# Low parts of the first block's attention and retention weights: every other one subtracted on GpSimd

## Chip, cores and metric

One core of a Trainium2 chip runs the kernel. The metric is the device time of one execution in microseconds, as the median of several runs. TensorE (PE; its weight loads are PEld), VectorE (DVE), ScalarE (ACT), GpSimd (POOL) and SyncE (SP, which starts the DMAs) each work through an instruction list of their own and wait for each other through semaphores.

## What is computed

Two transformer blocks in fp32 on x of 256 rows by 1024. The first block has two layers: an attention layer (layer 0) and a retention layer (layer 1), each followed by a gated feed-forward layer. A vector c gives each layer six modulation vectors ("ada"). The second block is two further hybrid layers, which the change doesn't touch.

```python
def first_block(x, c, ada_w, ada_b, norm_gains, ...):
    for layer in range(2):
        shift_m, scale_m, gate_m, shift_f, scale_f, gate_f = split(silu(c) @ ada_w[layer] + ada_b[layer], 6)
        h = rms_norm(x, norm_gains[layer, 0]) * (1 + scale_m) + shift_m
        y = attn_hybrid_mixer(h, ...) if layer == 0 else retention_mixer(h, ...)
        x = x + gate_m * y
        h = rms_norm(x, norm_gains[layer, 1]) * (1 + scale_f) + shift_f
        x = x + gate_f * swiglu(h, ...)
    return rms_norm(x, final_norm)

def attn_hybrid_mixer(h, w_qkv, w_o, pos):       # 16 heads of 64
    q, k, v = heads(h @ w_qkv)
    sb = stick_breaking_attention(q[:8], k[:8], v[:8])
    mb = moba_attention(rotary(q[8:]), rotary(k[8:]), v[8:])   # one block here: causal softmax
    return concat(sb, mb) @ w_o

def retention_mixer(h, w_in, gn_gain, w_o, pos): # 4 heads
    q, k, v, g = split(h @ w_in)
    o = group_norm(retention_chunkwise(rotary(q), rotary(k) * dk ** -0.5, v)) * gn_gain
    return (silu(g) * o) @ w_o
```

## The kernel before

Every matrix product is made of three products in the reduced type fp32r, from a high and a low part of each operand: high times high, low times high, high times low. The weights arrive in fp32 in raw tiles of 128 by 2048, which SyncE loads (`raw`, L320). Two raw buffers lie in the pool `wp`, and every third raw tile goes to a buffer in `lp`. `pump` (L334) cuts each raw tile, a "chunk", into two pieces of 128 by 1024. Of each piece ScalarE makes the high part, tile `whi`, by a cast (L350), and VectorE the low part, tile `wlo`, as raw minus high part (L351). There is a ring of WB = 8 pieces. `pump` is called as TensorE's products use pieces up, so it runs ahead of them by at most eight.

The order of TensorE's instructions is written by hand: the program keeps a clock of its own (`now`) and due times of jobs (`push`, `tick`), and under `manual_schedule` TensorE's instructions stand in the order in which this recording makes them. The other engines' orders are made by a scheduler of the language. A job such as `rotary` or `causal_job` is a generator: what stands behind a `yield D_...` is recorded that many microseconds of the recorder's clock later.

Beside the gemms run background steps: the modulation vectors. `ada_steps` (L564) clears a 128 by 1024 accumulator on GpSimd (L566), loads the bias row into it (L567), and adds eight products of a 128 by 1024 weight slab with a per-partition scalar, each one a VectorE instruction (L575, "acc step"). There is one accumulator buffer, so a vector's memset waits for the split of the vector before (L491, L492). `pump` feeds such steps at a rate per chunk, `R_L0` = 2.04 in layer 0 and `R_L1` = 0.59 in layer 1.

Layer 0 (`layer0`, L823): behind the startup come the stick-breaking heads (`sb_job`, L655: tiles `sbe`, `sbs` and `aT`, the second and third of which VectorE finishes at L666, L668 and L674), while the gemm of the rotated heads' q and k runs. Its results go through `rotary` on VectorE (L616 to L619: tiles `rows` and `rt`), are transposed on TensorE (L284) and copied to qT and kT on ScalarE (L865). Then come the heads with causal softmax (`causal_job`, L621: the masked maximum on VectorE at L632, tiles `sm` and `st`, the exponential and the scaling on ScalarE, L636 and L640), while the v gemm runs, and the gemm of `w_ao`. `split` at L492 makes the low part of a head's output, tile `oTk`.

Layer 1 (`layer1`, L989): the gemms of q and k with `rotary` behind each, then those of v, then those of the gate g; the heads' group norm takes a `rstd` (L484), whose power is a GpSimd instruction on 128 by 1 (L487); then the gemm of `w_ro`. GpSimd has little else to do in the kernel: these powers, those of the other norms (L519), and the memsets.

## Time and profile before

| what | value |
| --- | --- |
| runs shown | 1473.52, 1475.32, 1475.45 us; median 1475.32 |
| the profiled execution's own time | 1474.96 us |
| its span (first to last instruction) | 1473.0 us, granted TensorE clock 0.995 on average |
| TensorE busy | 98% |
| VectorE, ScalarE, GpSimd busy | 71%, 55%, 7% |
| low parts, VectorE L351 | 450 instructions, 538.2 us |
| acc steps, VectorE L575 | 80 instructions, 102.2 us |

The profile is one execution taken apart by engine. Busy time is the sum over an engine's instructions; the idle time that counts is TensorE's, and it is told stage by stage by windows and by the timeline, in which an idle stretch of an engine stands in brackets with the work that ended it. All times in the trace are counted from the start of the span. A row of the timeline that ends in x2 is two equal instructions, one behind the other.

### The profile page before, as it was taken

The page shows a single profiled execution, that of the slowest core. Times are in us where ns is not written, and L with a number is a line of the kernel's source. Part 1 is how long each engine was busy: PE and PEld are TensorE (multiplying, and loading weights), DVE is VectorE, ACT ScalarE, POOL GpSimd, SP SyncE. Part 2 cuts the span into 40 slices and gives each one's busy share as a digit, 9 for nine tenths or more (in the row PEclk, how much of TensorE's full clock was granted, in tenths as well). Part 3 has the DMA queues.
Part 4 walks back from the last instruction along what each step waited for, and adds up shares of the span by engine and source line. Part 5 has one row for each costly group of instructions (what it writes and reads, how often), then busy time and mean ns, then how long its engine had stood idle before and what let it go on. Part 6 is the DMA issues. An engine that isn't in the chain of part 4 may idle for free.

```text
span 1473.0 us, 19815 instructions
## 1 busy us (share of the span) xinstructions
PE 1448.8 (98%) x7476; PEld 1185.7 (80%) x7476; DVE 1046.3 (71%) x1675; ACT 813.6 (55%) x1365; POOL 106.4 (7%) x88
## 2 busy tenths in 40 slices
PE   8999999999999999999999999999999999999998
PEld 6776788887887888888878888888888888888887
DVE  5688898956988848966378756565666866666664
ACT  4657556643544535655356755666445675566651
POOL 0000000000001000000012012110000201221000
PEclk9999999999999999999999999999999999999999
DMA  9757587765776646755435455455535545555452
GB/s 380 280 201 271 199 315 287 286 207 184 284 272 243 235 165 233 297 185 197 165 123 194 166 184 210 162 177 172 193 143 190 188 147 206 195 188 189 158 175 82
DMA packets 53091, 306.64 MB, mean 208 GB/s; under 512 B 7674, under 2 KB 12154, under 8 KB 20100
## 3 DMA queue, kind: packets, MB, share of 16 engines
q1 hardware_dynamic: 51988, 304.87, 57.8%
q8 instruction: 59, 0.97, 0.3%
q10 hardware_dynamic: 1008, 0.50, 0.1%
q14 instruction: 36, 0.29, 0.1%
HBM read 301.16 MB, written 1.05 MB: 205 GB/s over the span
## 4 chain that ended last, share of the span: by engine, by line
PE 88%; DVE 5%; ACT 2%; DMA 2%; POOL 1%; issue 1%; ACTq 0%; DVEq 0%; POOLq 0%
PE p L280 84%; PE p L284 4%; DVE wlo L351 2%; ACT whi L350 1%; DMA raw<-in_w_in_dram 1%; POOL qss L487 1%; POOL ss L519 0%; DMA as<-in_ada_s_dram 0%; DVE junk L527 0%; DMA sq<-in_k_sq_dram 0%; DVE res L554 0%; DMA raw<-in_w_ao_dram 0%; DVE acc L575 0%; DVE x L555 0%; ACT sm L636 0%
## 5 line engine op out<-in xcount | busy, mean ns | idle before, releaser
L280 PE MATMUL p<-whi,hT 128*128 128x512 f32 (+1 forms) x2240 | 748.1, 401 | 4.9 <-DVE hT L492 2.7
L351 DVE TENSOR_TENSOR wlo<-raw,whi 128x1024 fp32r<-128x1024 f32 x450 | 538.2, 1215 | 147.9 <-ACT whi L350 143.9
L350 ACT CAST whi<-raw 128x1024 fp32r<-128x1024 f32 x450 | 461.8, 1045 | 242.7 <-PE p L280 189.4
L280 PEld LDWEIGHTS p<-whi,hT 128*128 128x128 f32 x2240 | 422.8, 189 | 99.7 <-issue 7.3
L280 PE MATMUL p<-wlo,hT 128*128 128x512 f32 (+1 forms) x1120 | 437.6, 391 | 0.0
L280 PEld LDWEIGHTS p<-wlo,hT 128*128 128x128 f32 x1120 | 212.1, 189 | 39.2 <-issue 1.7
L280 PE MATMUL p<-hT,whi 128*128 128x512 f32 x576 | 199.2, 398 | 0.0
L280 PE MATMUL p<-hT,wlo 128*128 128x256 f32 x576 | 149.9, 281 | 0.0
L280 PEld LDWEIGHTS p<-hT,whi 128*128 128x128 f32 x576 | 103.8, 188 | 19.6
L280 PEld LDWEIGHTS p<-hT,wlo 128*128 128x128 f32 x576 | 108.7, 189 | 6.6
L575 DVE SCALAR_TENSOR_TENSOR acc<-raw,csc,acc 128x1024 f32<-128x1024 f32 x80 | 102.2, 1277 | 3.5 <-DMA raw<-in_ada_w_dram 3.2
L487 POOL TENSOR_TENSOR dss<-dss,mh 128x8 f32<-128x8 f32 (+3 forms) x36 | 56.1, 1557 | 318.2 <-DVE dss L486 318.2
L280 PE MATMUL p<-whi,al 128*128 128x512 f32 x176 | 69.5, 395 | 0.0
L280 PE MATMUL p<-wlo,ah 128*128 128x512 f32 x176 | 69.5, 395 | 0.0
L280 PE MATMUL p<-whi,ah 128*128 128x512 f32 x176 | 69.5, 395 | 0.0
L1410 DVE TENSOR_TENSOR rows<-p,dss 128x512 f32<-128x512 f32 (+3 forms) x36 | 18.5, 514 | 46.2 <-POOL dss L487 46.2
L962 ACT COPY fT<-p 128x256 f32<-128x256 f32 x72 | 26.2, 370 | 45.2 <-PE p L280 45.2
L519 POOL TENSOR_TENSOR ss<-ss,mh 128x1 f32<-128x1 f32 x14 | 13.4, 960 | 471.2 <-DVE ss L518 471.2
L280 PE MATMUL p<-whi,s 128*128 128x512 f32 x128 | 41.3, 397 | 0.0
L280 PEld LDWEIGHTS p<-wlo,ah 128*128 128x128 f32 x176 | 33.0, 187 | 8.1
L280 PEld LDWEIGHTS p<-whi,al 128*128 128x128 f32 x176 | 33.0, 187 | 8.0
L280 PEld LDWEIGHTS p<-whi,ah 128*128 128x128 f32 x176 | 33.0, 187 | 8.0
(262 smaller groups left out, 1621.1 us busy)
## 6 DMA issues: line engine op xcount, KB each, us to landing
raw<-in_w_in_dram SPq DMA_DIRECT2D x84, 1024.0 KB, 4.9
raw<-in_w_gu_dram SPq DMA_DIRECT2D x44, 1024.0 KB, 5.2
raw<-in_ada_w_dram SPq DMA_DIRECT2D x40, 1024.0 KB, 5.3
raw<-in_w_ret_dram SPq DMA_DIRECT2D x24, 1024.0 KB, 4.9
raw<-in_w_dn_dram SPq DMA_DIRECT2D x22, 1024.0 KB, 4.9
raw<-in_w_qkv_dram SPq DMA_DIRECT2D x11, 1024.0 KB, 5.7
as<-in_ada_s_dram SPq DMA_DIRECT2D x16, 512.0 KB, 10.0
raw<-in_w_ro_dram SPq DMA_DIRECT2D x8, 1024.0 KB, 6.1
```

The costliest lines, as they stand in the source:

```text
L280: self.T.matmul(out, lhsT=lhsT, rhs=rhs, start=first, stop=last, skip_group_check=skip)
L284: self.T.transpose(out, in_, self.ident)
L350: for ins in (self.A.copy(hi[:, :m * n], src), self.V.tensor_tensor(lo[:, :m * n], src, hi[:, :m * n].bitcast(F32), ALU.subtract)):
L351: self.V.tensor_tensor(lo[:, :m * n], src, hi[:, :m * n].bitcast(F32), ALU.subtract)):
L487: self.G.tensor_tensor(ss, ss, self.mh[:, :n], ALU.pow)
L519: self.G.tensor_tensor(ss[:, 0:1], ss[:, 0:1], self.mh[:, 0:1], ALU.pow)
L575: self.V.scalar_tensor_tensor(acc, r[:, j * D:j * D + D], self.sc[:, k:k + 1], acc, ALU.mult, ALU.add)
L962: A.copy(f, ps[:, 256:512])
L1410: V.tensor_tensor(d3(rows[:, :nu * 128]), d3(src), ss[:, :2 * nu, None].to_broadcast([128, 2 * nu, 64]), ALU.mult)
```

## The change

A flag `share` is false at first. It is set behind layer 0's startup and cleared ahead of the gemm of `w_ao`; set again at the head of layer 1 and cleared ahead of the gemm of `w_ro`. While it is set, `pump` gives the subtraction of the second piece of each chunk (j = 1) to GpSimd; the first stays on VectorE. The cast stays on ScalarE for both.

```diff
--- before.py
+++ after.py
@@ -249,6 +249,7 @@
         self.tc, self.nc, self.a, self.ctx = tc, tc.nc, a, ctx
         nc = tc.nc
         self.T, self.V, self.A, self.G = nc.tensor, nc.vector, nc.scalar, nc.gpsimd
+        self.share = False
         self.base = ctx.enter_context(tc.tile_pool(name="base", bufs=1))
         self.wp = ctx.enter_context(tc.tile_pool(name="wp", bufs=WB))
         self.hp = ctx.enter_context(tc.tile_pool(name="hp", bufs=1))
@@ -347,8 +348,10 @@
                 hi = self.wp.tile([128, 1024], F32R, tag="whi", name=self.nm("whi"))
                 lo = self.wp.tile([128, 1024], F32R, tag="wlo", name=self.nm("wlo"))
                 src = r[:, k * n:(k + m) * n]
+
+                sub = self.G if self.share and j % 2 else self.V
                 for ins in (self.A.copy(hi[:, :m * n], src),
-                            self.V.tensor_tensor(lo[:, :m * n], src, hi[:, :m * n].bitcast(F32), ALU.subtract)):
+                            sub.tensor_tensor(lo[:, :m * n], src, hi[:, :m * n].bitcast(F32), ALU.subtract)):
                     if self.pin:
                         self.tc.keep_in_program_order(ins)
                 v = lambda w: w[:, :m * n].rearrange("p (k n) -> p k n", n=n)
@@ -826,7 +829,7 @@
             self.ph, self.smb = p, 3
             hT, ps0 = self.startup(lp)
             self.tc.keep_in_program_order(A.preload_act_table_set("natural_log_exp_and_others"))
-            self.rate = R_L0
+            self.rate, self.share = R_L0, True
             jobs = [self.ada(lp, 0, v) for v in (2, 3, 4)]
             rope = p.tile([128, 2, 3, 32], F32, name="rope64")
             nc.sync.dma_start(rope, self.a["k_rope64"].rearrange("p (t j d) -> p t j d", t=2, j=3))
@@ -902,6 +905,7 @@
                 return tuple(x[:, k % 4, t * 128:t * 128 + 128] for x in oT[k // 4])
 
             nxt = self.res_norm(gate, lambda: self.finish(jobs[1], jobs[2])[::-1])
+            self.share = False
             self.gemm_k(ho, "w_ao", 8, nxt.epi, tail=T_AO)
         return nxt
 
@@ -993,7 +997,7 @@
             nc.sync.dma_start(rope, self.a["k_rope256"].rearrange("p (t j d) -> p t j d", t=2, j=3))
             dec = p.tile([128, 4, 384], F32, tag="dg", name="decay")
             nc.sync.dma_start(dec, self.a["k_decay"].rearrange("p (h n) -> p h n", h=4))
-            self.rate = R_L1
+            self.rate, self.share = R_L1, True
             jobs = [self.ada(lp, 1, v) for v in (2, 3, 4)]
             s4 = lambda dt=F32: p.tile([128, 4, 256], dt, tag="s4", bufs=9, name=self.nm("s4"))
             as_rows = lambda x: x.rearrange("p a b -> p (a b)").rearrange("p (t n) -> p t n", t=2)
@@ -1083,6 +1087,7 @@
                 return tuple(x[:, k % 4, t * 128:t * 128 + 128] for x in oT[k // 4])
 
             nxt = self.res_norm(gate, lambda: self.finish(jobs[1], jobs[2])[::-1])
+            self.share = False
             self.gemm_k(ho, "w_ro", 16, nxt.epi)
         return nxt
```

All later lines of the changed program stand one to five lines further down: L351 becomes L354, L575 becomes L578, rotary's L616 to L619 become L619 to L622, and so on. Thirty subtractions change engine, six in layer 0 and 24 in layer 1. TensorE's order is the same in both programs. VectorE's, ScalarE's and SyncE's are made anew by the scheduler, and change beyond the thirty. Three places follow.

VectorE, late in the stick-breaking heads of layer 0, up to the rotation of the first q rows (`rows_901`), which TensorE transposes next. `acc_800` is the first modulation vector's accumulator, `raw_808`, `raw_893` and `raw_897` its weight slabs, `aT_776` a stick-breaking head's tile. First an earlier piece of it, before:

```order
L575 SCALAR_TENSOR_TENSOR acc_800<-raw_808,csc,acc_800 128x1024
L351 TENSOR_TENSOR wlo_793<-raw_790,whi_792 128x1024
L351 TENSOR_TENSOR wlo_797<-raw_790,whi_796 128x1024
L575 SCALAR_TENSOR_TENSOR acc_800<-raw_808,csc,acc_800 128x1024
L616 TENSOR_TENSOR rows_901<-p_766,rope_645 128x512
L575 SCALAR_TENSOR_TENSOR acc_800<-raw_893,csc,acc_800 128x1024
L666 SCALAR_TENSOR_TENSOR sbs_754<-p_750,sbe_753 128x384
```

and now:

```order
L578 SCALAR_TENSOR_TENSOR acc_800<-raw_808,csc,acc_800 128x1024
L354 TENSOR_TENSOR wlo_793<-raw_790,whi_792 128x1024
L578 SCALAR_TENSOR_TENSOR acc_800<-raw_808,csc,acc_800 128x1024
L578 SCALAR_TENSOR_TENSOR acc_800<-raw_893,csc,acc_800 128x1024
L619 TENSOR_TENSOR rows_901<-p_766,rope_645 128x512
L578 SCALAR_TENSOR_TENSOR acc_800<-raw_893,csc,acc_800 128x1024
L669 SCALAR_TENSOR_TENSOR sbs_754<-p_750,sbe_753 128x384
```

The low part `wlo_797` is gone, and the second of the two acc steps on `raw_893` stands here, where before it came later. The piece that ends with the rotation's last add, before:

```order
L351 TENSOR_TENSOR wlo_886<-raw_883,whi_885 128x1024
L351 TENSOR_TENSOR wlo_890<-raw_883,whi_889 128x1024
L575 SCALAR_TENSOR_TENSOR acc_800<-raw_893,csc,acc_800 128x1024
L617 TENSOR_TENSOR rt_902<-p_766,rope_645 128x8x32
L575 SCALAR_TENSOR_TENSOR acc_800<-raw_897,csc,acc_800 128x1024
L618 TENSOR_TENSOR rt_902<-p_766,rope_645 128x8x32
L575 SCALAR_TENSOR_TENSOR acc_800<-raw_897,csc,acc_800 128x1024
L619 TENSOR_TENSOR rows_901<-rows_901,rt_902 128x512
```

and now:

```order
L354 TENSOR_TENSOR wlo_886<-raw_883,whi_885 128x1024
L578 SCALAR_TENSOR_TENSOR acc_800<-raw_897,csc,acc_800 128x1024
L620 TENSOR_TENSOR rt_902<-p_766,rope_645 128x8x32
L578 SCALAR_TENSOR_TENSOR acc_800<-raw_897,csc,acc_800 128x1024
L621 TENSOR_TENSOR rt_902<-p_766,rope_645 128x8x32
L677 SCALAR_TENSOR_TENSOR aT_776<-aT_776,strict 128x2x128
L622 TENSOR_TENSOR rows_901<-rows_901,rt_902 128x512
```

The low part `wlo_890` and the acc step on `raw_893` are gone from here, and one stick-breaking product, `aT_776`, now stands ahead of the last add instead of behind it.

GpSimd, from the first memset to the sixth low part, before:

```order
L566 MEMSET acc_800 128x1024
L519 ISA
L519 TENSOR_TENSOR ss_131<-ss_131,mh 128x1
L519 TENSOR_TENSOR ss_150<-ss_150,mh 128x1
L566 MEMSET acc_991 128x1024
L566 MEMSET acc_1226 128x1024
L566 MEMSET acc_1673 128x1024
```

and now:

```order
L354 TENSOR_TENSOR wlo_797<-raw_790,whi_796 128x1024
L354 TENSOR_TENSOR wlo_890<-raw_883,whi_889 128x1024
L569 MEMSET acc_991 128x1024
L354 TENSOR_TENSOR wlo_984<-raw_977,whi_983 128x1024
L354 TENSOR_TENSOR wlo_1028<-raw_1021,whi_1027 128x1024
L354 TENSOR_TENSOR wlo_1219<-raw_1212,whi_1218 128x1024
L569 MEMSET acc_1226 128x1024
L354 TENSOR_TENSOR wlo_1306<-raw_1299,whi_1305 128x1024
L569 MEMSET acc_1673 128x1024
```

The six low parts of layer 0 stand between what was there, and the memset of the third accumulator, `acc_1226`, now stands behind `wlo_1219`.

VectorE, at the first softmax head (tiles `sm_1098`, `st_1099`; `acc_991` is the second accumulator), before:

```order
L492 TENSOR_TENSOR oTk_1050<-p_1058,oTq_1049 128x256
L351 TENSOR_TENSOR wlo_1024<-raw_1021,whi_1023 128x1024
L351 TENSOR_TENSOR wlo_1028<-raw_1021,whi_1027 128x1024
L575 SCALAR_TENSOR_TENSOR acc_991<-raw_1031,csc,acc_991 128x1024
L492 TENSOR_TENSOR oTk_1050<-p_1065,oTq_1049 128x256
L575 SCALAR_TENSOR_TENSOR acc_991<-raw_1031,csc,acc_991 128x1024
L492 TENSOR_TENSOR oTk_1050<-p_1072,oTq_1049 128x256
L575 SCALAR_TENSOR_TENSOR acc_991<-raw_1035,csc,acc_991 128x1024
L632 ISA sm_1098,st_1099<-p_1095,causal_647 128x128
L632 ISA st_1099 128x1
L575 SCALAR_TENSOR_TENSOR acc_991<-raw_1035,csc,acc_991 128x1024
L632 ISA sm_1098,st_1099<-p_1095,causal_647 128x256
```

and now:

```order
L354 TENSOR_TENSOR wlo_1024<-raw_1021,whi_1023 128x1024
L495 TENSOR_TENSOR oTk_1050<-p_1058,oTq_1049 128x256
L495 TENSOR_TENSOR oTk_1050<-p_1065,oTq_1049 128x256
L495 TENSOR_TENSOR oTk_1050<-p_1072,oTq_1049 128x256
L578 SCALAR_TENSOR_TENSOR acc_991<-raw_1031,csc,acc_991 128x1024
L635 ISA sm_1098,st_1099<-p_1095,causal_647 128x128
L635 ISA st_1099 128x1
L578 SCALAR_TENSOR_TENSOR acc_991<-raw_1031,csc,acc_991 128x1024
L635 ISA sm_1098,st_1099<-p_1095,causal_647 128x256
L635 ISA st_1099 128x1
```

The low part `wlo_1028` is gone, and of the four acc steps that stood ahead of the head's second maximum two are left.

## Rows read from the trace of the kernel before

**Rows 1.** The page's first part: busy time of each engine over the span.
```profile
PE 1448.8 (98%) x7476; PEld 1185.7 (80%) x7476; DVE 1046.3 (71%) x1675; ACT 813.6 (55%) x1365; POOL 106.4 (7%) x88
```
**Rows 2.** Windows (start:end, length, busy time of each engine, PEclk, DMA share, GB/s).
```profile
128.00:144.00 16.00, 13.96 (x67) 9.82 (x66) 15.32 (x41) 15.43 (x45) 0.00 (x0) 1.00 0.65 215
...
375.00:530.00 155.00, 155.00 (x698) 124.22 (x697) 133.09 (x163) 74.00 (x90) 8.30 (x11) 1.00 0.70 257
```
**Rows 3.** Timeline of PE, layer 0 (start, duration; in brackets idle before, releaser).
```profile
94.62 0.66 PE L284 MATMUL p<-ident,rows 128*128 128x128 f32 x2 [3.38 <-DVE rows L619]
...
112.20 0.63 PE L284 MATMUL p<-ident,rows 128*128 128x128 f32 x4 [0.33 <-DVE rows L619]
...
131.75 0.84 PE L284 MATMUL p<-ident,sm 128*128 128x128 f32 x3 [0.70 <-ACT sm L640]
```
**Rows 4.** Windows around PE's longest idle stretch in layer 0 (PEclk: granted clock).
```profile
91.24:94.60 3.36, 0.00 (x0) 0.01 (x1) 3.36 (x5) 1.19 (x2) 0.00 (x0) 0.85 0.98 378
94.60:97.00 2.40, 2.38 (x8) 2.11 (x9) 2.02 (x4) 0.94 (x2) 0.32 (x1) 0.50 1.00 355
97.00:99.50 2.50, 2.50 (x7) 1.92 (x7) 1.19 (x3) 0.00 (x0) 0.63 (x1) 0.50 0.80 329
99.50:102.00 2.50, 2.50 (x13) 2.11 (x12) 1.27 (x3) 0.85 (x2) 0.00 (x0) 0.82 0.12 49
```
**Rows 5.** Timeline of DVE up to the same stretch's end.
```profile
75.96 1.22 DVE L351 TENSOR_TENSOR wlo<-raw,whi 128x1024 fp32r<-128x1024 f32 x1
...
84.56 0.56 DVE L666 SCALAR_TENSOR_TENSOR sbs<-p,sbe 128x384 f32<-128x384 f32 x1 [0.43 <-PE p L280]
...
87.27 2.35 DVE L351 TENSOR_TENSOR wlo<-raw,whi 128x1024 fp32r<-128x1024 f32 x2
89.54 1.28 DVE L575 SCALAR_TENSOR_TENSOR acc<-raw,csc,acc 128x1024 f32<-128x1024 f32 x1
90.74 0.42 DVE L617 TENSOR_TENSOR rt<-p,rope 128x256 f32<-128x256 f32 x1
...
93.79 0.68 DVE L619 TENSOR_TENSOR rows<-rows,rt 128x512 f32<-128x512 f32 x1
94.39 0.75 DVE L674 SCALAR_TENSOR_TENSOR aT<-aT,strict 128x256 f32<-128x256 f32 x2
```
**Rows 6.** Groups of lines by form, POOL: memset of an accumulator.
```profile
L566 POOL MEMSET acc<- 128x1024 f32 x10 | 9.6, 956 | 329.0 <-DVE accl L492 218.6 <-DMA raw<-in_ada_w_dram 88.2 <-issue 21.9
```
**Rows 7.** Timeline of POOL, two powers of layer 1, and DVE beside the second.
```profile
431.65 0.55 POOL L487 TENSOR_TENSOR bn<-bn,mh 128x1 f32<-128x1 f32 x1 [19.11 <-DVE bn L486]
435.59 1.59 POOL L487 TENSOR_TENSOR bn<-bn,mh 128x1 f32<-128x1 f32 x1 [3.39 <-DVE bn L486]
...
435.54 1.23 DVE L351 TENSOR_TENSOR wlo<-raw,whi 128x1024 fp32r<-128x1024 f32 x1
```
**Rows 8.** All of L351: ns min/median/max; below it, who waited for it.
```profile
L351 DVE TENSOR_TENSOR wlo<-raw,whi x450: 957/1220/1230, 13.5 to 1450.0; 128x1024 fp32r<-128x1024 f32 x144, 128x832 fp32r<-128x832 f32 x4, 128x768 fp32r<-128x768 f32 x2
...
  ACT whi L350: 1.1, 1
```
**Rows 9.** Timelines of DVE, ACT and PE around the second rotation of layer 0.
```profile
105.06 1.22 DVE L351 TENSOR_TENSOR wlo<-raw,whi 128x1024 fp32r<-128x1024 f32 x1
...
111.26 1.05 ACT L350 CAST whi<-raw 128x1024 fp32r<-128x1024 f32 x1 [1.24 <-DMA raw<-in_w_ao_dram]
...
113.79 0.48 PE L280 MATMUL p<-kT,qT 64*128 64x256 f32 x1 [0.55 <-ACT kT L865]
```
**Rows 10.** Timelines of DVE and ACT at the first softmax head.
```profile
120.73 0.42 DVE L632 CUSTOM_DVE_ANT_0 sm<-p,causal 128x256 f32<-128x256 f32 x1
...
122.71 0.40 ACT L636 ACTIVATE sm<-sm,st 128x128 f32<-128x128 f32 x1
```
**Rows 11.** Timelines of DVE and PE, a rotation in layer 1.
```profile
389.25 0.68 DVE L619 TENSOR_TENSOR rows<-rows,rt 128x512 f32<-128x512 f32 x1
...
392.48 0.60 PE L284 MATMUL p<-ident,rows 128*128 128x128 f32 x4
```

## The prediction

> **What bounds the kernel now.** The page's busy times come first [rows 1]: TensorE is busy for 98% of the span, and VectorE, the engine that the change relieves, for 71%. So the time can only move where TensorE stands still, or comes to. Next the windows [rows 2]: in the stretch of layer 1 shown TensorE is busy for 155.00 of 155 us, in layer 0's softmax heads for 13.96 of 16, so 2.04 us are idle there. The timeline of TensorE in layer 0 [rows 3] names the idle times: 3.38 us that end at 94.62 with the rotated rows from VectorE, 0.33 at 112.20 with the second rotation's rows, and in the softmax pieces of up to 0.70, of which ScalarE's scaled `sm` ends the longest. The clock must be read with the first of these [rows 4]: it is granted at 0.85 on average in the idle stretch, then at 0.50 while TensorE is fully busy again from 94.60 to 99.50, and at 0.82 in the next window. If in that last window it rises once from 0.5 to 1, 0.36 of its 2.50 us, 0.9 us, are at 0.5: 5.8 us at half clock (1.2 instead of 2.4 GHz), so 2.9 us of work lost.
>
> Is a low part itself late for TensorE? Over all 450 subtractions only ScalarE ever waits for one, once, for 1.1 us [rows 8]. The low parts are made ahead of need. What VectorE's subtractions cost is the place they take ahead of the rotated rows and the softmax tiles.
>
> **Two unknowns.** The trace shows no GpSimd subtraction of this size. Let t be its time. The nearest row is the memset of the same 128x1024 shape, one stream (a write): 0.956 us [rows 6]. A subtraction reads two tiles and writes one. Low bound: the memset's 0.95. High bound: three streams one behind the other, 2.85. I take two, 1.9: the write runs beside the reads, the reads one behind the other, as with a single path.
>
> The second unknown is whether VectorE's instructions wait while GpSimd's runs. The only hint is a pair of powers on 128x1 [rows 7]: alone one took 0.55 us; the other began 0.05 us behind the start of a VectorE subtraction of 1.23 us, and took 1.59, that is 0.41 longer than the rest of the subtraction (1.18) and about the sum of that rest and its own work. So GpSimd stood until VectorE was done. The other direction, VectorE standing until GpSimd is done, is not shown. I take it to hold too: one path to memory that one of the two has at a time. Then a piece moved to GpSimd costs VectorE t instead of the 1.14 us from one of its subtractions to the next (88.41 being half way in the pair that begins at 87.27 and ends before 89.54 [rows 5]), so each moved piece is 0.76 us dearer.
>
> The Trainium skill ("SBUF — State Buffer", Who interferes with whom) says that a VectorE instruction with two SBUF inputs contends with a GpSimd instruction that reads SBUF, and that whoever has the shared port pair first keeps it for the whole instruction while the other stands. The 0.55 against 1.59 us agree on GpSimd's side; no row shows VectorE's.
>
> **The change part by part.** Thirty subtractions leave VectorE. ScalarE's casts and the loads stay; their order moves.
>
> *A, the idle stretch before 94.62.* The order decides how much VectorE does ahead of `rows_901`'s last add. In the earlier piece `wlo_797` (−1.14) leaves and an acc step moves in (+1.20, 89.54 to 90.74 [rows 5]): +0.06, plus t if VectorE is held, less the 0.43 us that VectorE idles at 84.56 and can absorb. In the later piece `wlo_890` (−1.13) and that acc step (−1.20) leave and one `aT` product comes in (+0.33, from 94.39: two take 0.75, less overlap): −2.00, plus t. With holding: 0.06 + t − 0.43 − 2.00 + t = 2t − 2.37. At t = 1.9 that is **+1.43**; at 0.95 −0.47; at 2.85 +3.33. The half clock behind it I leave as it is, since the idle stretch is hardly shorter at the low bound (2.91) and longer at the others.
>
> *B, the second rotation.* `wlo_984` leaves the stretch in which VectorE makes the second rows (it is the subtraction at 105.06 or its pair [rows 9]), and its raw buffer `raw_977` is read until GpSimd is done. Behind that buffer stand a load of `w_ao`, for which ScalarE idles 1.24 us at 111.26, and the copy of kT behind it, for which TensorE waits 0.55 at 113.79 [rows 9]. Either way the shift is t − 1.14 = **+0.76**. Bounds: −0.33, the idle time at 112.20 being all there is to win, and +1.71 at t = 2.85. On SyncE the load of another weight tile now goes ahead of that of `raw_977`, some pieces ahead of use: nothing.
>
> *C, the softmax heads.* Before the first head's second maximum at 120.73 [rows 10], two acc steps and `wlo_1028` less: 2 × 1.20 + 1.14 − t = 1.64 us earlier, and ScalarE's first scaling at 122.71 can come earlier with it. TensorE has 2.04 us idle there [rows 2], on ScalarE's work, which is itself busy 15.43 of 16. I take half: **−1.0**; bounds 0 and −2.04.
>
> *D, the third accumulator.* Its memset now stands behind `wlo_1219` on GpSimd; behind the memset come SyncE's bias row, the first acc step and VectorE's small instructions after it. A memset that comes t later than it would delays acc steps that no TensorE work needs for many pieces: **0**, up to +1 if a softmax reciprocal stands behind such a waiting acc step.
>
> *E, layer 1, 24 pieces.* TensorE has no idle time to win [rows 2]. VectorE has 155 − 133.09 = 21.91 us idle in the stretch; 24 × 0.76 = 18.2 us dearer would still fit, if spread evenly. The tightest consumer is the rotation: rows done at 389.25 + 0.68 = 389.93, transposed at 392.48 [rows 11], 2.55 us to spare. Three moved pieces near it would cost 3 × 0.76 = 2.3, just inside: **0**; at t = 2.85 3 × 1.71 = 5.13, less the 2.27 for two subtractions that no longer stand ahead, less 2.55, is +0.3. The group norm's powers wait behind at most one piece, and the gate gemm lies between them and their use.
>
> Sum: +1.43 + 0.76 − 1.0 + 0 + 0 = **+1.2 us** on the profiled execution's 1474.96, so 1476.2. That execution is 0.36 below the median of the runs shown; on the median, 1475.32 + 1.2 = **1476.5**.
>
> The Trainium skill ("GPSIMD Engine Reference", 3.1 Elementwise) speaks against the change: it gives 4497 ns on GpSimd and 2293 on VectorE for a fp32 tensor_tensor of 2048 elements. Halved, an estimate from that page is t = 2.25; the sum would be 3 × 2.25 − 3.51 − (2.40 + 1.14 − 2.25) / 1.64 × 1.0, about +2.5, or 1477.8. No run here shows it.
>
> This case's own range is 1473.5 (t at 0.95 with all of C) to 1479.5 (t toward 2.85, C still won in part).
>
> **Rivals.**
>
> *F, VectorE isn't held.* The two engines share memory access finely, or only GpSimd yields. For it: no VectorE subtraction in 450 took over 1.230 us [rows 8], though GpSimd was at work beside some of them; and in the pair shown it was GpSimd that stood. Against: those GpSimd instructions were tiny. Then A is −2.00, the idle stretch 1.38 us; that may leave the clock up, −2.9; B −0.33; C −1.0: together −6.2, so **1469.1**. If the clock falls all the same, −3.3, 1472.0.
>
> *S, slower: GpSimd holds VectorE, and long.* One mechanism: each low part on GpSimd stops VectorE's two-input instructions, just ahead of the rotated rows. A and B together are 3t − 3.51; without C they pass 2.95 us, about what a measurement of this kernel can tell from no change (0.2%), from t = 2.15 on. At t = 2.85: 3.33 + 1.71, C gone (0), D +1, E +0.3, so +6.3 and **1481.7**. For it: two reads and a write are three streams, and the idle stretch before 94.62 is VectorE's alone. Against: A's two pieces may begin in VectorE's idle times or beside instructions that read one tile. By the Trainium skill's rule ("SBUF — State Buffer", Who interferes with whom) this case comes about if t is that long; the trace bears it out in one direction alone.
>
> That the change does nothing can be left out: thirty subtractions stand on GpSimd in the order.
>
> **Chances.** Forecast case (about no change) 0.42, F 0.33, S 0.25. The first lies mostly within 0.2%, a little of it above; F is faster but for a small part where the clock falls and B is not won; S is slower but for its lower edge. So faster 0.32, within 0.2% 0.40, slower 0.28. The range takes F from its full price and S to its own: 1468.5 to 1482.0.
>
> **What would show it.** GpSimd's 128x1024 subtraction at 0.95, 1.9 or 2.85 us. VectorE's two-input instructions beside it stretched or late by its length (held), or still at 1.22 and 1.28 (F). The idle stretch that ended at 94.62: 4.8 us long (forecast), under 1.5 (F), over 6 (S), and the granted clock behind it. The 2.04 us between 128 and 144 halved. Layer 1 still without idle time on TensorE. I am wrong if layer 1 gains or loses over 1 us, or if a low part is itself waited for by TensorE.

## The result, and the profile after

The changed kernel takes 1493.88 us (median of 4 runs, 1492.25 to 1494.76) beside 1474.49 us for the kernel before in the same comparison: a ratio of 1.0128, interval 1.0116 to 1.0141, or 19 us slower. That is above the range (1468.5 to 1482.0). The side on which it fell is rival S's, at three times its price.

Busy times of the whole span first, as in [rows 1]. The profiled execution took 1494.76 us, its span 1493.0.

```profile
PE 1456.3 (98%) x7476; PEld 1189.1 (80%) x7476; DVE 1065.2 (71%) x1645; ACT 811.5 (54%) x1365; POOL 188.9 (13%) x118
```

VectorE has 30 instructions fewer here and is busy 18.9 us longer. Why, the changed instructions tell: the group of the 30 on GpSimd, and then, from the views of single lines, five VectorE lines (ns min/median/max).

```profile
L354 POOL TENSOR_TENSOR wlo<-raw,whi 128x1024 fp32r<-128x1024 f32 x30 | 84.5, 2829 | 172.6 <-ACT whi L353 172.6
...
L354 POOL TENSOR_TENSOR wlo<-raw,whi x30: 2361/2816/3438, 78.1 to 534.5; 128x1024 fp32r<-128x1024 f32 x30
...
L354 DVE TENSOR_TENSOR wlo<-raw,whi x420: 957/1220/3428, 13.3 to 1469.9; 128x1024 fp32r<-128x1024 f32 x134, 128x832 fp32r<-128x832 f32 x4, 128x768 fp32r<-128x768 f32 x2
L578 DVE SCALAR_TENSOR_TENSOR acc<-raw,csc,acc x80: 1264/1278/3405, 70.0 to 622.6; 128x1024 f32<-128x1024 f32 x80
L1053 DVE TENSOR_TENSOR s<-s,gn x8: 684/1366/2881, 446.6 to 497.1; 128x512 f32<-128x512 f32 x8
...
L619 DVE TENSOR_TENSOR rows<-p,rope x12: 676/682/692, 68.0 to 417.7; 128x512 f32<-128x512 f32 x12
L1052 DVE TENSOR_SCALAR s<-p,bn x8: 799/810/812, 445.7 to 494.3; 128x512 f32<-128x512 f32 x8
```

A low part on GpSimd takes 2.36 us at least, 2.83 on average and 3.44 at most. On VectorE, three of the lines shown have instructions drawn out to 2.9 to 3.4 us; before, no subtraction took over 1.230 [rows 8]. These three read two big tiles in SBUF. The two lines that take their big operand from PSUM (`p`) are never drawn out, though three instructions of each lie wholly within a low part on GpSimd in the trace. Averages by shape give the size: 408 subtractions of 128x1024 at 1.269 instead of 1.221 us are 19.6 us, 80 acc steps at 1.448 instead of 1.277 are 13.7, together 33 us, about what the 30 subtractions that left had cost (30 × 1.14 = 34). Three lines of 128x512 with two operands in SBUF (L1053, L622 and L1075: 1.68, 1.09 and 1.41 us on average instead of about 0.69) add 18.6 us. So being held cost VectorE more than it was relieved of, by about the 18.9 us.

One hold in full, from the timelines of GpSimd, VectorE and TensorE in layer 1:

```profile
515.22 3.38 POOL L354 TENSOR_TENSOR wlo<-raw,whi 128x1024 fp32r<-128x1024 f32 x1 [2.87 <-ACT whi L353]
...
515.09 1.27 DVE L578 SCALAR_TENSOR_TENSOR acc<-raw,csc,acc 128x1024 f32<-128x1024 f32 x1
516.28 3.39 DVE L354 TENSOR_TENSOR wlo<-raw,whi 128x1024 fp32r<-128x1024 f32 x1
519.60 0.68 DVE L1075 TENSOR_TENSOR gth<-gth,s 128x512 f32<-128x512 f32 x1
...
520.34 0.47 PE L285 MATMUL p<-ident,gth 128*128 128x128 f32 x1 [3.00 <-DVE gth L1075]
```

GpSimd's piece starts at 515.22 while an acc step runs to 516.36, and ends at 518.60, 2.24 us behind that step. VectorE's next subtraction starts at 516.28 and ends at 519.67, 1.07 behind GpSimd's end. Each stands until the other is done. Behind VectorE stands the product `gth`, and TensorE waits 3.00 us for it. This agrees, now in both directions, with the Trainium skill's rule ("SBUF — State Buffer", Who interferes with whom) on the shared port pair.

TensorE's idle times, from its timeline in both layers, and windows of stretches with and behind them (columns as in [rows 2, 3]):

```profile
86.31 0.92 PE L281 MATMUL p<-sbs,sq 128*128 128x256 f32 x4 [1.56 <-DVE sbs L671]
...
97.76 0.63 PE L285 MATMUL p<-ident,rows 128*128 128x128 f32 x4 [3.52 <-DVE rows L622]
...
113.64 0.63 PE L285 MATMUL p<-ident,rows 128*128 128x128 f32 x4 [1.32 <-DVE rows L622]
115.67 0.70 PE L281 MATMUL p<-kT,qT 64*128 64x256 f32 x2 [0.99 <-ACT kT L868]
...
463.34 1.22 PE L281 MATMUL p<-s,raT 128*128 128x512 f32 x1 [4.08 <-ACT s L1059]
```
```profile
94.20:97.80 3.60, 0.08 (x2) 0.07 (x2) 3.60 (x7) 1.53 (x2) 0.00 (x0) 1.00 0.82 264
97.80:100.40 2.60, 2.60 (x14) 2.20 (x15) 2.20 (x4) 0.59 (x1) 0.92 (x1) 1.00 1.00 413
...
118.50:122.80 4.30, 4.30 (x11) 2.75 (x10) 4.30 (x11) 0.00 (x0) 0.00 (x0) 0.50 0.89 332
463.00:468.00 5.00, 4.66 (x9) 3.04 (x10) 5.00 (x4) 4.56 (x6) 4.07 (x3) 0.50 0.49 194
520.00:527.00 7.00, 6.66 (x19) 5.44 (x20) 7.00 (x7) 5.44 (x7) 5.10 (x3) 0.55 0.68 269
...
375.00:530.00 155.00, 147.92 (x640) 116.93 (x639) 138.00 (x134) 64.96 (x82) 68.98 (x33) 0.96 0.64 236
```

Layer 1, gapless before [rows 2], now has two idle stretches, 4.08 and 3.00 us, each with a stretch at half clock behind it, and TensorE is busy for 147.92 of the 155 us instead of all of them. TensorE's own instructions, one by one, tell where the 20 us came: the first transpose of layer 0's norm began at 163.18 before and at 169.41 now (+6.2, of which 1.4 stood there before the first moved piece); the one at 507 before, some way into layer 1's gate gemm, comes 19.4 later, and from there on that moves by no more than about 1.5 us. So layer 1 lost 13 us in this execution. The two idle stretches are 7.1 of them (155 less 147.92); the half clock behind them is the rest.

The first idle stretch of layer 1 is not as plain as the second. Its pieces, from the timelines of GpSimd, VectorE and ScalarE, in order of time within each engine, and below them the two ScalarE instructions of the kernel before that correspond to the last two:

```profile
418.94 2.79 POOL L354 TENSOR_TENSOR wlo<-raw,whi 128x1024 fp32r<-128x1024 f32 x1 [6.37 <-ACT whi L353]
421.68 0.94 POOL L569 MEMSET acc<- 128x1024 f32 x1
...
424.35 1.28 DVE L578 SCALAR_TENSOR_TENSOR acc<-raw,csc,acc 128x1024 f32<-128x1024 f32 x1 [2.07 <-DMA acc<-in_ada_b_dram]
...
438.40 1.23 DVE L354 TENSOR_TENSOR wlo<-raw,whi 128x1024 fp32r<-128x1024 f32 x1 [3.84 <-ACT whi L353]
439.84 3.13 DVE L578 SCALAR_TENSOR_TENSOR acc<-raw,csc,acc 128x1024 f32<-128x1024 f32 x1 [0.21 <-DMA raw<-in_ada_w_dram]
...
461.76 1.04 ACT L494 CAST acch<-acc 128x1024 fp32r<-128x1024 f32 x1 [12.46 <-DVE acc L578]
462.71 0.58 ACT L1059 COPY s<-p 128x512 f32<-128x512 f32 x1
```
```profile
445.22 0.59 ACT L1055 COPY s<-p 128x512 f32<-128x512 f32 x1 [6.56 <-PE p L280]
446.44 1.05 ACT L491 CAST acch<-acc 128x1024 fp32r<-128x1024 f32 x1 [0.63 <-DVE acc L575]
```

The accumulator's memset stands behind a low part on GpSimd; its bias row, and so the first acc step, come late; the next steps are held; the raw tiles that they read come free late, and with them the casts. At the end the cast of the finished accumulator waits on ScalarE for its last acc step, and the copy of a head's v, ready long before, stands behind it in ScalarE's list. For that copy TensorE waits. In the kernel before the copy stood ahead of the cast: the scheduler has turned the two round. So by these rows this idle stretch needs both, an accumulator that is late and the new order.

### The profile page after: what moved, and what is told of

It is laid out like the page before. It is cut to its first block, busy times and chain, and to the rows that moved or that the text cites. A ratio compares the mean times of both kernels' runs of the same rounds, so it can differ in the third digit from the quotient of the medians.

```text
span 1493.0 us, 19848 instructions
## 1 busy us (share of the span) xinstructions
PE 1456.3 (98%) x7476; PEld 1189.1 (80%) x7476; DVE 1065.2 (71%) x1645; ACT 811.5 (54%) x1365; POOL 188.9 (13%) x118
## 4 chain that ended last, share of the span: by engine, by line
PE 77%; DVE 12%; DMA 4%; issue 3%; ACT 2%; POOL 2%; ACTq 0%; DVEq 0%; POOLq 0%; SPq 0%
PE p L281 73%; DVE wlo L354 4%; PE p L285 4%; DVE acc L578 3%; DMA raw<-in_w_in_dram 1%; ACT whi L353 1%; DMA raw<-in_ada_w_dram 1%; POOL qss L490 1%; DMA raw<-in_w_ret_dram 1%; DVE s L1053 1%; DMA sq<-in_k_sq_dram 0%; DMA as<-in_ada_s_dram 0%; DVE junk L530 0%; POOL ss L522 0%; POOL wlo L354 0%
## 5 line engine op out<-in xcount | busy, mean ns | idle before, releaser
L354 DVE TENSOR_TENSOR wlo<-raw,whi 128x1024 fp32r<-128x1024 f32 x420 | 522.5, 1261 | 142.9 <-ACT whi L353 140.2
L578 DVE SCALAR_TENSOR_TENSOR acc<-raw,csc,acc 128x1024 f32<-128x1024 f32 x80 | 115.8, 1448 | 11.0 <-DMA raw<-in_ada_w_dram 8.6
L281 PEld LDWEIGHTS p<-hT,whi 128*128 128x128 f32 x576 | 103.8, 188 | 19.6
L354 POOL TENSOR_TENSOR wlo<-raw,whi 128x1024 fp32r<-128x1024 f32 x30 | 84.5, 2829 | 172.6 <-ACT whi L353 172.6
```

Of the source, the lines that this page charges most:

```text
L281: self.T.matmul(out, lhsT=lhsT, rhs=rhs, start=first, stop=last, skip_group_check=skip)
L354: sub.tensor_tensor(lo[:, :m * n], src, hi[:, :m * n].bitcast(F32), ALU.subtract)):
L578: self.V.scalar_tensor_tensor(acc, r[:, j * D:j * D + D], self.sc[:, k:k + 1], acc, ALU.mult, ALU.add)
```

## The experiments

Two theories were left after this reading, and a third had to be excluded: HOLD, QUEUE and ORDER, as the first expectation names them. All the kernels below keep TensorE's order, but for the last two; the other engines' orders are made anew by the scheduler in each. Times are medians; each comparison had its own runs of the kernel before, 1474.8 to 1474.9 us in all three.

**One layer at a time.**

```diff
-            self.rate, self.share = R_L1, True
+            self.rate = R_L1
```

> The flag is set in layer 0 only: 6 of the 30 low parts on GpSimd. Three theories. HOLD: a GpSimd low part stops every VectorE instruction with two operands in SBUF until it is done, and the held instructions reach TensorE late. QUEUE: it is the things that stand behind the low parts, the accumulator's memset on GpSimd, with it the bias row's load on SyncE, and the raw buffers that come free late. ORDER: it is the new order of VectorE, ScalarE and SyncE. By the two traces TensorE's instructions at the end of layer 0's norm came 6.2 us later, 1.1 of which had been there before the first moved piece. All three theories: about +5 us over before, 1479 to 1480; this run only splits the loss by layer. If the loss of layer 1 were a follow-up of layer 0's, it would stay near +19.

Measured: 1484.36 us, ratio 1.0067 (1.0045 to 1.009), 9.5 us slower. The opposite edit, in layer 0:

> The flag is set in layer 1 only: 24 of the 30 low parts on GpSimd. By the two traces layer 1 lost 13.4 us, in two idle stretches of TensorE of 4.08 and 3.00 us and the half clock behind each. All theories that see the layers apart: about +13.5 us, 1488. If the idle stretches hang on when exactly pieces meet, anything between +5 and +16.

Measured: 1484.93 us, ratio 1.0072 (1.0045 to 1.01), 10.1 us slower. The layers' losses add up to the whole, 19.6 of 19.4 us, and neither is a follow-up of the other. Layer 0's is larger than the trace of the changed kernel alone had it, layer 1's smaller: the 1479 to 1480 expected for the first was missed, and the second is within its wide range alone (+5 to +16). The window of layer 1 in the first and in the second:

```profile
375.00:530.00 155.00, 155.00 (x701) 124.42 (x700) 135.72 (x170) 74.62 (x89) 8.30 (x11) 1.00 0.71 259
```
```profile
375.00:530.00 155.00, 147.77 (x644) 116.59 (x643) 138.42 (x129) 66.73 (x84) 73.64 (x35) 0.98 0.65 239
```

**GpSimd busy as long, but only writing.**

```diff
-                sub = self.G if self.share and j % 2 else self.V
...
+                if self.share and j % 2:
+                    self.A.copy(hi[:, :m * n], src)
+                    self.G.tensor_tensor(lo[:, 0:1], src[:, 0:1], hi[:, 0:1].bitcast(F32), ALU.subtract)
+                    for _ in range(3):
+                        self.G.memset(lo[:, :m * n].bitcast(F32), 0.0)
+                    self.G.tensor_tensor(lo[:, 0:1], src[:, 0:1], hi[:, 0:1].bitcast(F32), ALU.subtract)
```

> The low part of the 30 moved pieces is left out but for its first column; in its place GpSimd clears the tile three times, 3 x 0.95 = 2.9 us (the moved subtractions took 2.83 on average), between two subtractions of one column, so it begins behind the cast and keeps the raw tile as long as before. What goes is GpSimd's reading of two big tiles. HOLD: VectorE's two-operand instructions keep their 1.22 and 1.28 us, and the time is that of before or less, 1470 to 1478. QUEUE: the memset, the bias row and the raw buffers wait as long as in the changed kernel, so at least +10, 1485 or more. ORDER: VectorE's order is nearly that of the changed kernel, so +15 or more.

Measured: 1483.81 us, ratio 1.0058 (1.0037 to 1.008), 9 us slower. No theory alone has this. VectorE's subtractions, layer 1's window, from the timelines of TensorE, GpSimd, SyncE and ScalarE the place in layer 0 where most of the loss is, and at the end two ScalarE instructions of layer 1:

```profile
L361 DVE TENSOR_TENSOR wlo<-raw,whi x420: 957/1224/1254, 13.5 to 1459.3; 128x1024 fp32r<-128x1024 f32 x134, 128x832 fp32r<-128x832 f32 x4, 128x768 fp32r<-128x768 f32 x2
```
```profile
375.00:530.00 155.00, 154.88 (x699) 123.92 (x698) 110.39 (x145) 72.08 (x89) 93.16 (x131) 1.00 0.70 254
```
```profile
93.96 0.63 PE L285 MATMUL p<-ident,rows 128*128 128x128 f32 x4 [1.57 <-ACT acch L502]
...
113.76 0.79 PE L281 MATMUL p<-kT,qT 64*128 64x256 f32 x1 [2.91 <-ACT kT L876]
...
106.17 0.19 POOL L357 TENSOR_TENSOR wlo<-raw,whi 128x1 fp32r<-128x1 f32 x1
...
95.70 0.33 SPq L329 DMA_DIRECT2D raw<-in_w_ao_dram  x1
106.39 0.34 SPq L329 DMA_DIRECT2D raw<-in_w_ao_dram  x1
...
111.23 1.04 ACT L360 CAST whi<-raw 128x1024 fp32r<-128x1024 f32 x1 [4.56 <-DMA raw<-in_w_ao_dram]
...
454.72 0.59 ACT L1067 COPY s<-p 128x512 f32<-128x512 f32 x1 [5.84 <-PE p L281]
461.12 1.05 ACT L502 CAST acch<-acc 128x1024 fp32r<-128x1024 f32 x1 [3.97 <-DVE acc L586]
```

Without GpSimd's reading of big tiles no subtraction on VectorE is drawn out (1.254 at most), and layer 1 loses nothing, though GpSimd is as long at work there, the raw tiles are kept as long and the memsets stand behind it. So QUEUE alone costs layer 1 nothing in this kernel, which speaks for HOLD. It doesn't exclude ORDER: the scheduler has put the accumulator's cast (461.12) behind the copy (454.72) again, as before the change, and the subtraction that stood directly ahead of `gth` stands elsewhere. The two places where the changed kernel loses aren't there to be tested.

In layer 0 the idle stretch before the first rotated rows shrinks from 3.38 to 1.57 us, the relief at work. But loads of `w_ao` start at 95.70 and 106.39, just when GpSimd is done with a raw tile (at 95.67 and 106.36). For the second of them ScalarE idles 4.56 us, the copy of kT stands behind its casts, and TensorE stands 2.91; behind that the granted clock is 0.50 from 113.70 to 118.50. The run overstates the queue a little: one of the one-column subtractions stood behind VectorE itself and took 2.69 us.

**The same, raw tile free early.** The second subtraction of one column is taken out, so the raw tile is no longer kept to the end.

> As the run with GpSimd's writes alone, but without the second subtraction of one column, which kept the raw tile until the three memsets were done: the raw buffers come free as early as ScalarE and VectorE and one short GpSimd instruction let them. In that run the raw loads of layer 0 came late (a load of w_ao started at 95.70, when GpSimd was done, instead of 89.65), ScalarE's casts behind them, and behind these the copy of kT for which TensorE waited 2.91 us. QUEUE for layer 0 (raw buffers freed late): that 2.91 us falls to about 0.5 and the half clock behind it goes, some 6 us won, 1475 to 1478. If the loss of layer 0 is of the memsets alone, it stays at 1482 or more.

Measured: 1475.57 us, ratio 1.0003 (0.9991 to 1.0014): no difference from before. Two rows of TensorE's timeline in layer 0:

```profile
92.45 0.63 PE L285 MATMUL p<-ident,rows 128*128 128x128 f32 x4 [1.56 <-ACT acch L501]
...
109.61 1.28 PE L281 MATMUL p<-kT,qT 64*128 64x256 f32 x4 [0.26 <-ACT kT L875]
```

One row of SyncE's timeline in this run, and below it two from GpSimd's and SyncE's in the changed kernel, for the same chain:

```profile
100.37 0.34 SPq L329 DMA_DIRECT2D raw<-in_w_ao_dram  x1
```
```profile
104.61 3.23 POOL L354 TENSOR_TENSOR wlo<-raw,whi 128x1024 fp32r<-128x1024 f32 x1 [4.17 <-ACT whi L353]
...
107.86 0.33 SPq L329 DMA_DIRECT2D raw<-in_w_ao_dram  x1
```

The load that started at 106.39 starts at 100.37, the 2.91 us are 0.26, and 8.2 us are won. A raw tile kept longer, six times, by three memsets and a column (3.2 to 5.8 us) is enough for a loss as large as layer 0's. VectorE's order differs somewhat between the two runs too, but the chain is seen directly, and the changed kernel has it: GpSimd's low part ends at 107.84, the load starts at 107.86, and the 0.99 us for the copy of kT follow.

And the relief, free of these costs, is worth nothing at the end. TensorE's instruction that began at 100.41 before begins at 95.55 here, 4.9 us earlier, the one at 131.75 only 1.7 earlier. Of the 4.9 only 1.8 are the shorter idle stretch (1.56 for 3.38). Most of the rest is the half clock that the kernel before had behind it [rows 4] and this run hasn't (1.00 on average from 90 to 108).

**Memsets on VectorE**, first in the changed kernel, then in the run just told:

```diff
-        self.G.memset(acc, 0.0)
+        (self.V if self.share else self.G).memset(acc, 0.0)
```

> The changed kernel, with the accumulators' memsets on VectorE instead of GpSimd while the flag is set: the memset, and the bias row's load behind it, no longer stand behind low parts. The run with GpSimd's writes alone lost nothing in layer 1 though its memsets stood behind as long a stretch on GpSimd, and lost 9 us in layer 0. HOLD (layer 1's loss is VectorE held): layer 1 keeps most of its 10 to 13 us, layer 0 wins 1 to 3, so 1488 to 1493. QUEUE (the late memset starts layer 1's loss): the first idle stretch of layer 1, 4.08 us and its half clock, goes too, so 1482 to 1486.

Measured: 1497.33 us, ratio 1.015 (1.0124 to 1.0177): no gain, and neither range has it. TensorE's two idle stretches of layer 1 are still there:

```profile
462.84 0.86 PE L281 MATMUL p<-s,raT 128*128 128x512 f32 x1 [2.95 <-ACT s L1059]
...
519.69 0.55 PE L285 MATMUL p<-ident,gth 128*128 128x128 f32 x3 [2.96 <-DVE gth L1075]
```

The first is 1.1 us shorter in this execution; the late memset was a small part of it.

> As the run before, and the accumulators' memsets on VectorE while the flag is set. What is left of the change is VectorE's relief and its new order, with no hold, no raw buffer kept and no memset behind GpSimd's work. If hold and queue are all of the loss, the relief shows: the idle stretch before the rotated rows is under 2 us, and the time 1468 to 1474. If the new order costs something by itself, 1477 or more.

Measured: 1477.82 us, ratio 1.0019 (1.0005 to 1.0032), a miss for HOLD and QUEUE as all of the loss: 1468 to 1474 was expected of them. It lies where a cost of the new order was expected, 1477 or more, and is only just clear of no change. Its profiled execution is its fastest (1473.35), so no trace shows where such a cost would be.

**The hold without the relief.** VectorE subtracts all pieces, and behind it GpSimd does the 30 again.

> VectorE keeps all its subtractions, and GpSimd makes the 30 a second time behind VectorE, onto the same tile: the hold without the relief. HOLD: VectorE has 30 x 1.14 = 34 us more to do in the same stretches than in the changed kernel and is held as often, so worse than it: +25 to +45, 1500 to 1520. QUEUE: as the changed kernel, about +19. ORDER: the order is near to that of before, so within 3 us of it.

Measured: 1515.91 us, ratio 1.0273 (1.024 to 1.0305), 41 us slower, as HOLD had it. TensorE is busy for 136.92 of the 155 us of layer 1's window. ScalarE has the accumulator's cast behind the copy here, as before the change (486.75 and 470.04), so that reversal isn't needed for a loss. But the run doesn't part HOLD from the kept raw tile: GpSimd reads it behind VectorE, so it is kept for both.

**One operand read.** GpSimd copies the high part and then the raw tile onto the low part's tile.

> The low part of the 30 moved pieces is left out; in its place GpSimd copies first the high part and then the raw tile onto it: one operand read and one written, twice. If any reading by GpSimd of a big tile holds VectorE's two-operand instructions, they stretch beside these copies as in the changed kernel and layer 1 loses, in proportion to the copies' length (two of 1.0 to 1.9 us): 1484 to 1494. If only GpSimd's two-operand reading holds them, layer 1 loses nothing, and the time is near that of the writes alone, 1480 to 1485, with no stretched instruction on VectorE.

Measured: 1483.47 us, ratio 1.0053 (1.0032 to 1.0074). The copies, and VectorE's subtractions:

```profile
L354 POOL CAST wlo<-whi x30: 1031/1396/2142, 78.0 to 523.7; 128x1024 fp32r<-128x1024 f32 x30
...
L359 DVE TENSOR_TENSOR wlo<-raw,whi x420: 957/1224/2064, 13.5 to 1458.9; 128x1024 fp32r<-128x1024 f32 x134, 128x832 fp32r<-128x832 f32 x4, 128x768 fp32r<-128x768 f32 x2
```

Reading one operand holds VectorE too (up to 2.06 us), each time by a shorter copy. Yet TensorE is busy for all 155 us of layer 1's window, so the loss there that the first expectation wanted doesn't come: holds of this size find slack in this order (the accumulator's cast, at 457.51, stands behind the copy, at 453.99, as before the change). The 9 us are layer 0's: TensorE's instructions are 8.9 us late behind that layer's norm (1.3 of them from ahead of the first moved piece) and 8.8 at the end of layer 1.

**Short holds.** Four strips of 128x256 in place of a piece; every other engine's order is the changed kernel's.

```diff
+                    for c in range(0, m * n, 256):
+                        sl = slice(c, c + 256)
+                        self.G.tensor_tensor(lo[:, sl], src[:, sl], hi[:, sl].bitcast(F32), ALU.subtract)
```

> The changed kernel with each of the 30 low parts on GpSimd made in four strips of 128x256 instead of one piece; the order on every other engine is that of the changed kernel. HOLD, as it was read from the changed kernel: a VectorE instruction stands until the GpSimd instruction under way is done, so at most about 0.6 instead of 2.4 us at a time, and it can go between two strips. The sum of GpSimd's work is the same or more. If the length of a single hold is what made layer 1 late, layer 1's loss falls to under 4 us and the time is 1478 to 1486; GpSimd's strips themselves then wait for VectorE between each other. If only the sum of the reading counts, it stays within 3 us of the changed kernel, 1491 to 1497. QUEUE: the raw tiles are kept as long or longer, so layer 0's loss of 5 to 7 us stays in both cases.

Measured: 1495.49 us, ratio 1.0137 (1.0122 to 1.0152): nothing is won. The strips, VectorE's subtractions, and TensorE's timeline:

```profile
L356 POOL TENSOR_TENSOR wlo<-raw,whi x120: 719/1176/1772, 77.7 to 544.8; 128x256 fp32r<-128x256 f32 x120
...
L360 DVE TENSOR_TENSOR wlo<-raw,whi x420: 958/1224/1765, 13.5 to 1472.8; 128x1024 fp32r<-128x1024 f32 x134, 128x832 fp32r<-128x832 f32 x4, 128x768 fp32r<-128x768 f32 x2
...
117.11 1.22 PE L281 MATMUL p<-kT,qT 64*128 64x256 f32 x2 [3.88 <-ACT kT L875]
...
461.99 1.22 PE L281 MATMUL p<-s,raT 128*128 128x512 f32 x1 [4.99 <-ACT s L1066]
```

A held subtraction is shorter (1.77 us at most), and both idle stretches that the changed kernel had in layer 1 are gone, in the same order. That speaks for the length of the single hold as a cause of them, though TensorE comes there 8 us later. For GpSimd now stands for VectorE between strips: one takes 0.72 us at best and 1.18 in the median, so a piece 4.7 instead of 2.8, and the raw tile is kept that much longer. A new idle stretch of 4.99 us comes one product ahead of the old first one, for a copy that stands behind casts for which ScalarE waits 6.61 us (for a load). What VectorE doesn't wait, GpSimd does.

**The relief by another way.** The kernel before with the modulation steps of layer 0 fed at another rate, nothing on GpSimd.

```diff
-R_L0, R_FFN, R_L1 = 2.04, 0.65, 0.59
+R_L0, R_FFN, R_L1 = 1.9, 0.65, 0.59
```

> The kernel before, without any work moved to GpSimd, and with the modulation steps of layer 0 fed at 1.9 per chunk instead of 2.04. In its order on VectorE three acc steps stand behind the rotated rows' last add that stood ahead of it. This gives VectorE the relief that the change wanted, by another way. If the relief is worth what the runs with GpSimd's writes alone show up to the stretch behind the first rotation, 3 to 5 us, and no modulation vector is then waited for, 1469 to 1473. If the later steps are waited for at the end of layer 0, that takes it back: 1474 to 1478.

Measured: 1477.62 us, ratio 1.0018 (1.001 to 1.0027), slower by 2.8. The idle stretch before the first rotation is gone altogether, and TensorE is 6.9 us ahead at the first modulation vector's product (118.41 before, 111.53 here), the half clock of [rows 4] being gone too. At the first transpose of the norm 0.7 us are left (163.18 and 162.49). Two of the places that took it, from TensorE's timeline:

```profile
126.70 0.84 PE L284 MATMUL p<-ident,sm 128*128 128x128 f32 x3 [2.73 <-ACT sm L640]
...
154.54 0.49 PE L280 MATMUL p<-accl,ones_r 128*128 128x512 f32 x1 [1.96 <-DVE accl L492]
```

> The same with 1.5 per chunk: the relief is the same ahead of the first rotation, and the second and third accumulators come later still. Between the run with 1.9 and 4 us more; if a modulation vector is waited for in front of the norm of layer 0, over 1476.

Measured: 1483.69 us, ratio 1.0065 (1.0052 to 1.0078), slower by 9, and by 6 than the run with 1.9, where at most 4 were expected. No version here beats the kernel before.

## Why the prediction was wrong

**What held.** Low parts are hardly waited for by TensorE (one wait, 0.3 us); the hold works in both directions, as taken; and the change was on rival S's side by the mechanism named there, though not at the place named there (the rotated rows).

**t, mis-sized.** The forecast took 1.9 us, between one stream and three. The 30 took 2.83 on average, the upper bound (2.85). The shortest took 2.36. The estimate from the Trainium skill's page ("GPSIMD Engine Reference", 3.1 Elementwise), 2.25, was nearest to the shortest; the rest is GpSimd standing behind VectorE, which its own bound of three streams happened to cover. The memset was a poor neighbour for a price of reading.

**A.** With t = 2.83 the formula 2t − 2.37 gives 3.3 us. Idle time grew by 1.7: 0.14 at the old place (3.52 for 3.38) and 1.56 at a new one, at 86.31, where stick-breaking tiles stood behind a held acc step. That the half clock would stay was wrong: the clock is granted at 1.00 in and behind the stretch here, and so the place that the prediction feared most cost nothing in this execution: TensorE's instruction that began at 100.41 before begins at 100.86, 0.45 us later, where the delay had been 1.4 us ahead of the first moved piece. Why the clock fell behind 3.38 us in one execution and not behind 3.52 in another stays open.

**B.** t − 1.14 = 1.7 us, and the two idle times at 112 to 116 grew by 1.43. What the step left out is the half clock that came behind them (0.50 from 118.50 to 122.80), over 2 us. It named the raw buffer and the load of `w_ao`, but priced them as one and the same shift with VectorE's; the runs with writes alone show that a raw tile kept too long can by itself cost layer 0 some 8 of its 9 us.

**C.** A gain of 1.0 was forecast; idle time in the softmax heads grew by about 1.2 instead. A head start of TensorE in layer 0 is not kept: the run with raw tiles free and the one with another rate had 4.9 and 6.9 us of it and 1.7 and 0.7 a little later. So rival F, had its condition been met, would have given no gain either: its sum took a local gain for one at the end.

**E, the step that failed most.** It priced layer 1 at nothing from two sides: VectorE's 21.91 us of idle time, and 2.55 us to spare at the rotation. Layer 1 cost 10 us, where the prediction's own sign of being wrong was over 1. The first was worked out at t = 1.9 only; at the 2.83 measured, 24 × 1.69 = 40.6 us would not have fitted into 21.91. Yet VectorE is still idle for 17 of the 155 us now (138.00 busy), so that bound isn't what cost the time. The rotation was not the tightest consumer. Two others were: the gate's product `gth`, directly behind a held subtraction; and the finished accumulator's cast on ScalarE, ahead of a copy that TensorE needs, an order that the scheduler made with the change and that the prediction didn't look at. The step asked whether an engine's work fits, not what stands in line behind the longest single wait. And each of layer 1's two idle stretches brought a half clock that the sum had no term for.

**S.** Layer 0 came out near its price, partly by luck: 9.5 us measured by itself, some 5 in the changed kernel's own trace, against 6.0 for A, B and D, while A cost nothing there. Its +0.3 for layer 1 was the same error as E, which is why the range ended 12 us short.

What isn't settled: how much of layer 0's loss is HOLD. Taking the reading away leaves it as large, since the raw tile is then the limit, and no run has a piece that reads both tiles and frees the raw one early. Nor how much of layer 1's loss hangs on the scheduler's new order. The runs with a late accumulator cast ahead of the copy (the changed kernel, layer 1 alone, memsets on VectorE) lose there; those with the cast behind it (writes alone, one operand read) don't, and they are also those with no holds or shorter ones. The cast ahead of the copy costs nothing by itself: with the raw tiles free early it stands there too (442.68 and 444.14), and TensorE is busy for all 155 us.

## What to carry to other kernels

Before giving an engine with spare time a part of another's work, look whether the two share a path to memory: here the receiving engine was 93% idle and the giving engine ended 18.9 us busier, because each instruction that reads two big SBUF tiles on one stands until the other's is done. Price a move not by the engines' sums but by the longest single wait, by what stands behind it in every in-order list as the scheduler makes it anew (VectorE's, ScalarE's copies, the loads that need the buffer), and by the half clock that an idle stretch of TensorE may bring. And follow a local gain to the end of the stage before counting it.

## What the runs showed of the hardware

- GpSimd's 128x1024 subtraction in fp32: 2.36 us at best, against 1.22 on VectorE; a cast of that size 1.03 at best; a memset 0.95; a strip of 128x256 0.72.
- VectorE's instructions with two big SBUF operands and GpSimd's with one or two stand for each other (up to 3.43 us for 1.22). VectorE's with one operand from PSUM are not held (0.69 and 0.81 us at most), and GpSimd's memsets hold nothing: 90 of them left VectorE's longest subtraction at 1.254 us.
- The granted clock was 0.50 to 0.55 for several microseconds behind idle stretches of 3.38, 4.08, 3.00 and 2.91 us, and stayed at 1.00 behind one of 3.52 us.
